# A thirteenth column pair in the stage of seven quarter products, one plain unit ahead of the attention, and another dealing of filler matmuls

## The chip, the cores and the metric

The kernel runs on one core of a Trainium2 chip. A core has TensorE (PE, matrix products into PSUM, the accumulation memory), VectorE (DVE), ScalarE (ACT) and GpSimd (POOL), and SyncE (SP), whose queue issues nearly all DMAs here. Each engine works through its own instructions in order, and semaphores tie them together. The metric is the device time of one execution in microseconds (us); a second figure, the span, runs from the first to the last instruction of the program in the profiled execution.

## The reference

One layer of an encoder over 1024 new frames and 64 frames of a running stream (1088 columns in all), with 512 cached positions. All numbers are float32.

```python
h = rms_norm(x, norm_w) @ w_in                       # 1024 -> 6144 columns
sb_q, sb_k, sb_v, sb_z, cb_q, cb_k, cb_v, cb_z, g_sb, g_cb = split(h)
# sb: stick breaking, 8 heads x 64, causal over all earlier keys
A[t, s] = beta[t, s] * prod_{s<j<t} (1 - beta[t, j]),  beta = sigmoid(q.k / 8)
# cb: softmax over a band of 9 chunks of 64 keys with a relative bias
b_sb = (o_sb * silu(z_sb)) @ w_proj_sb ;  b_cb = (o_cb * silu(z_cb)) @ w_proj_cb
y = x + (sigmoid(g_sb) * b_sb + sigmoid(g_cb) * b_cb) @ w_out
```

The last 1024 columns of `w_in` are the gate g_cb: eight units of 128 columns. The gate g_sb is eight more.

## The kernel before

A float32 operand is cut into a high and a low part, and each product is three matmuls (high x high, high x low, low x high). The stages follow one another on PE:

1. Norm and the projections that need rows by token (up to 227.5 us in the profile).
2. The stage of pairs (line 625 on): `pairs` lists 12 pairs of 128-column units (k, q, the two z, and the eight units of g_sb as four pairs of kind "sig"). A pair is worked as a 2x2 block product in seven quarter products instead of eight, each of 4 x 3 matmuls over two column pieces (256 and 288), so 168 matmuls, with sums of operands and results on DVE. `emit` (565) evaluates a finished quarter: for "sig" an ACT sigmoid into an `hl` tile (four of them) and stores. The halves of the weights are loaded ahead by `load_raw`; after the last pair it loads unit 0 of the next list. `LEAD` = 5 quarter products lie between the cutting of a weight (`prep`, `presum`) and its use.
3. `units` lists the eight units of g_cb. `run_fill` (775) makes them in the plain way: three column chunks `ci` of 24 matmuls (two of 384 columns, one of 320), 72 a unit. When a chunk is done `ev_act` copies it out and stores it. At the first matmul of chunk 1 the next unit's weights are cut (`W.split`: ACT makes the high part, line 115, POOL the low one, 122) and those of the one after it are loaded. Its generator goes on into `proj_sb`, the projection of the sb output. These are the fillers: `fill(n)` (985) emits the next n of them wherever the schedule calls it.
4. Ahead of the attention (1174 on): six times `fill(24)`, then `flush()` (pending stores), then one load: q of the sample, k, q of the first columns, v and z.
5. The attention: 136 steps, 17 for each of four head pairs in sb, then in cb. Of a pair, step one is the sample (t = 8, 576 keys), then t = 0 to 7 (blocks of 128 queries), each for head 0 and head 1. In sb block t has 128(t+1) keys, in cb at most 640. In step i the program emits: (cb) the exponentials of step i-1 and the scaling of step i-2 on ACT; the scores of step i (`qk`, `z`, line 1033; the cb bias and minimum on DVE); (sb) the scan and product of step i-1 on DVE (`mid`, 1056, 1057), which make `be`; `flush`; half of the step's fillers; a value product that has come due (`av`, 1127, with the closing product by z on DVE, `zt`, 1132); the transposes of step i-3 (`tr`, 1088), copied out of PSUM by ACT or DVE (`wT`); the other half of the fillers. A value product comes due one step after the transposes of the sample, or of head 1 of an odd t.
6. The rest of the fillers while the last outputs are loaded, then `proj_cb` and the output product.

Filler counts per step came from the step's keys (`wt`), 336 for sb in all and 287 for cb. A gate holds fillers back in the last unit until the sb outputs are stored (`late["sb"]`, at t = 1, head 1 of the first cb pair): before, when the unit before the last is complete. In the last unit the outputs `d_o` are loaded (`load_og`) and cut by ACT and POOL or DVE (`og_hi`, `og_lo`) in the steps of the fillers (`og_step`).

Of the kernel before, what the change touches and what calls it, by code (L numbers as in the profile page):

```python
# [10 lines left out]
AF = mybir.ActivationFunctionType  # L11
# [6 lines left out]
KT = 8  # L18
# [14 lines left out]
def hybrid_step_kernel(ctx: ExitStack, tc: tile.TileContext, x_prompt, x_sample, c_sbk, c_sbv, c_cbk, c_cbv,  # L33
# [111 lines left out]
    pairs = []  # L145
# [4 lines left out]
    pairs += [("sig", 4096 + 128 * j, d_g["sb"][j:j + 2]) for j in range(0, KT, 2)]  # L150
    units = [("ev_act", 5120 + 128 * j, (AF.Copy, d_g["cb"][j])) for j in range(KT)]

# [391 lines left out]
    with ExitStack() as ph:  # L544
# [20 lines left out]
        def emit(i, w, half, c, src, ps):  # L565
# [209 lines left out]
    def run_fill():  # L775
        for j, (kind, c, args) in enumerate(units):
            wh, wl = W.sp.pop(("u", j))
            for ci, (a, b) in enumerate(CH):
                ps = psF.tile([128, 512], F32, name="acc")
                for k in range(KT):  # L780
                    for n, (w, x) in enumerate(((wh, 0), (wh, 1), (wl, 0))):
                        TE.matmul(ps[:, :b - a], w[:, k], xk(x, k)[:, a:b], start=k == 0 and n == 0,  # L782
                                  stop=k == KT - 1 and n == 2)
# [324 lines left out]
    def av(b, p, j):  # L1108
        o = psO.tile([128, 256], F32, name="o")
        vp, vs = VP[b, p]  # L1110
        if j == 4:
            nq = 64
            steps = [(kb, 0, 64) for kb in range(5)]
        else:
            nq = 256
            lo = 2 * j - 3 if b == "cb" else 0
            steps = [(kb, 0, 256) for kb in range(max(0, lo), 2 * j + 1)]
            if lo > 0:
                steps.append((lo - 1, 0, 128))
            steps.append((2 * j + 1, 128, 256))  # L1120
        base = wbase(b, j)
# [59 lines left out]
    n_sb = 72 * 5 - 24  # L1181
    n_cb = 72 * (len(units) - 2) - n_sb + FP
    wt = {"sb": lambda n: n, "cb": lambda n: n + 150}
    tot = {b: sum(wt[b](band(b, t)[1]) for bb, p, t, hd in seq if bb == b) for b in ("sb", "cb")}
    amount = {"sb": n_sb, "cb": n_cb}
    acc, emitted = 0.0, 0
    LAG = 3
    avq = []
    for i in range(len(seq) + LAG + 1):
        m = 0  # L1190
# [13 lines left out]
        if i < len(seq):  # L1204
            qk(i)
            if hd == 0:
                if t % 2 == 1 or t == 8 and (b, p) != ("sb", 0):
                    load_z(b, p, t // 2 if t < 8 else 4)
                prefetch(b, p, t)
            acc += amount[b] * wt[b](band(b, t)[1]) / tot[b]  # L1210
            if (b, p, t) == ("cb", 0, 8):
                acc += 12
            m = int(acc) - emitted
            emitted += m
        if 0 < i <= len(seq) and seq[i - 1][0] == "sb":
# [305 lines left out]
```

## Time and profile before

| | us |
|---|---|
| median of three runs | 986.17 (985.58 to 986.71) |
| the profiled execution | 986.78 |
| its span | 985.0 |
| stage of pairs, PE | 227.5 to 483.0 |
| plain units ahead of the attention, PE | 483.0 to 506.7 |
| sb attention, first scores to first cb scores | 506.7 to 673.6 |
| cb attention, to the last value product | 673.6 to 832 |

A row of a stretch gives its length, then busy time and, in brackets, the number of instructions of each engine. In the order of time a row is start, duration, engine, line, operation and tiles; in square brackets the idle time ahead of it and what ended it. PE's busy time includes the tail of each matmul, so that short waits are hidden in it. "PEld" is a weight load, "SPq" the issue of a DMA.

### The profile page before, as it was taken

To read this page: it belongs to the slowest core of one execution; us is meant where nothing else is said; L and a number is where in the kernel's file an instruction comes from. 1 tells how busy PE (TensorE), PEld (TensorE's weight loads), DVE (VectorE), ACT (ScalarE), POOL (GpSimd) and SP (SyncE) were. 2 spreads that over 40 slices of the span, in tenths; PEclk is the share of its full clock that TensorE was granted. 3 is DMA by queue.
4 is the path that set the end of the run, shared out by engine and by line. 5 is a ranking of instruction groups with operands and counts; after the bars stand their busy time and mean duration, and the time that the engine had idled before them with its cause. 6 is when DMAs were issued, how large, how long until landed. Compare 5 with 4: busy or idle time off the path is not lost.

```text
span 985.0 us, 20439 instructions
## 1 busy us (share of the span) xinstructions
PE 962.0 (98%) x7568; PEld 917.6 (93%) x7568; DVE 630.1 (64%) x1188; ACT 510.4 (52%) x1142; POOL 346.2 (35%) x356
## 2 busy tenths in 40 slices
PE   5999999999999999999999999999999999999998
PEld 5999999999999999999998888898888888999998
DVE  5456665696454655532239898997767765599735
ACT  5534443344443433433248787786876875466220
POOL 3376664115444554444211101101201101486641
PEclk9999999999999999999999999999999999999999
DMA  6727567533656333343298656666898772852642
GB/s 229 223 89 243 193 223 253 166 103 120 180 174 203 115 110 101 99 124 99 79 244 221 172 160 161 164 187 169 232 262 226 213 221 68 264 177 83 210 131 86
DMA packets 174243, 166.97 MB, mean 170 GB/s; under 512 B 34688, under 2 KB 160000, under 8 KB 174016
## 3 DMA queue, kind: packets, MB, share of 16 engines
q1 hardware_dynamic: 165424, 157.34, 53.7%
q10 hardware_dynamic: 8720, 8.33, 2.6%
q8 instruction: 60, 0.98, 0.4%
q14 instruction: 39, 0.32, 0.1%
HBM read 106.89 MB, written 58.72 MB: 168 GB/s over the span
## 4 chain that ended last, share of the span: by engine, by line
PE 90%; DMA 3%; ACT 3%; DVE 1%; SPq 1%; issue 1%; POOL 1%; DVEq 0%; ACTq 0%
PE b L634 25%; PE acc L464 19%; PE b L1435 8%; PE o L1127 7%; PE acc L782 7%; PE z L1033 6%; PE pt L1088 6%; PE b L924 5%; PE acc L882 3%; DMA wrawx<-in_w_in_dram 1%; PE pk L349 1%; ACT wT L1097 1%; PE pt L277 1%; SPq L51 1%; PE acc L1471 1%
## 5 line engine op out<-in xcount | busy, mean ns | idle before, releaser
L122 POOL TENSOR_TENSOR wlo<-wraw,whi 128x1024 fp32r<-128x1024 f32 x22 | 57.6, 2618 | 103.0 <-ACT whi L115 102.9
L1088 PE MATMUL pt<-ident,be 128*128 128x128 f32 (+1 forms) x568 | 87.2, 278 | 5.7 <-ACT wT L1097 1.9
L1056 DVE TENSOR_TENSOR_SCAN kp<-kp,imp 128x128 f32<-128x128 f32 (+7 forms) x64 | 88.3, 1379 | 0.6 <-ACT kp L1036 0.6
L1033 PE MATMUL z<-ks,sq 128*128 128x320 f32 (+5 forms) x384 | 83.2, 325 | 0.0
L1088 PEld LDWEIGHTS pt<-ident,be 128*128 128x128 f32 (+1 forms) x568 | 65.9, 140 | 16.8 <-issue 5.7
L1097 ACT ACTIVATE wT<-pt 128x512 f32<-128x512 f32 (+3 forms) x125 | 58.6, 501 | 39.0 <-PE pt L1088 38.9
L464 PE MATMUL acc<-whi,xa 128*128 128x256 f32 x256 | 74.2, 292 | 0.0
L464 PE MATMUL acc<-wlox,xm 128*128 128x256 f32 x256 | 70.8, 278 | 0.0
L464 PE MATMUL acc<-whi,xm 128*128 128x256 f32 x256 | 70.8, 278 | 0.0
L464 PE MATMUL acc<-wlo,xa 128*128 128x256 f32 x256 | 70.7, 278 | 0.0
L464 PE MATMUL acc<-whix,xb 128*128 128x256 f32 x256 | 70.7, 278 | 0.0
L464 PE MATMUL acc<-whix,xm 128*128 128x256 f32 x256 | 70.6, 278 | 0.0
L1033 PEld LDWEIGHTS z<-ks,sq 128*128 128x128 f32 x384 | 65.8, 188 | 1.1 <-issue 0.2
L1127 PE MATMUL o<-wT,vp 128*64 128x256 f32 (+1 forms) x608 | 66.7, 357 | 0.1
L782 PE MATMUL acc<-xm,whi 128*128 128x384 f32 (+1 forms) x192 | 65.2, 340 | 0.0
L1127 PEld LDWEIGHTS o<-wT,vp 128*64 128x64 f32 x608 | 42.3, 136 | 23.9 <-issue 5.7
L1057 DVE TENSOR_TENSOR be<-be,kp 128x128 f32<-128x128 f32 (+8 forms) x68 | 57.3, 843 | 9.4 <-ACT sg L757 0.5
L1036 ACT ACTIVATE kp<-z 128x384 f32<-128x384 f32 (+6 forms) x104 | 52.4, 504 | 9.5 <-PE z L1033 4.5
L642 DVE TENSOR_TENSOR u<-b,s 128x256 f32<-128x256 f32 (+1 forms) x48 | 20.8, 439 | 56.3 <-PE b L634 55.2
L1037 ACT ACTIVATE be<-z 128x384 f32<-128x384 f32 (+6 forms) x104 | 52.9, 508 | 0.0
L1060 ACT ACTIVATE be<-be,sm 128x640 f32<-128x640 f32 (+5 forms) x68 | 47.2, 694 | 9.5 <-DVE sm L1059 9.2
L1047 ACT ACTIVATE be<-be,sm 128x640 f32<-128x640 f32 (+5 forms) x68 | 47.2, 694 | 3.7 <-DVE sm L1039 3.4
(300 smaller groups left out, 3147.4 us busy)
## 6 DMA issues: line engine op xcount, KB each, us to landing
wraw<-in_w_in_dram SPq DMA_DIRECT2D x32, 512.0 KB, 4.6
wrawx<-in_w_in_dram SPq DMA_DIRECT2D x16, 512.0 KB, 4.5
sq<-d_qsbT SPq DMA_DIRECT2D x32, 192.0 KB, 3.6
sq<-d_qcbT SPq DMA_DIRECT2D x32, 192.0 KB, 4.4
xt<-in_x_prompt_dram SPq DMA_DIRECT2D x8, 512.0 KB, 5.8
d_kcbT<-hl SPq DMA_DIRECT2D x8, 512.0 KB, 4.4
d_qcbT<-hl SPq DMA_DIRECT2D x8, 512.0 KB, 5.7
d_ksbT<-hl SPq DMA_DIRECT2D x16, 256.0 KB, 2.5
```

The lines of the kernel that those rows point to most:

```text
L122: (eng or G).tensor_tensor(out=l, in0=raw, in1=h[:].bitcast(F32), op=OP.subtract)
L464: TE.matmul(ps, x, w, start=m == 0, stop=m == len(steps) - 1)
L634: TE.matmul(ps[:, :m], w[:, hl_, k], right[s](x)[:, k, a:b], start=s < 3 and k == 0 and e == 0, stop=k == 3 and e == 2, skip_group_check=s ...
L782: TE.matmul(ps[:, :b - a], w[:, k], xk(x, k)[:, a:b], start=k == 0 and n == 0, stop=k == KT - 1 and n == 2)
L1033: TE.matmul(z[:, :m], s[:, e, q0:q0 + 128], ks[:, h, o + x:o + y], start=e == parts[0][0], stop=e == parts[-1][0])
L1037: A.activation(be[:r, x:y], z[:r, :m], AF.Sigmoid, scale=0.125)
L1056: V.tensor_tensor_scan(kp[:r, n - 1::-1], kp[:r, n - 1::-1], im[:, ::-1], 0.0, op0=OP.mult, op1=OP.add)
L1057: V.tensor_tensor(out=be[:r, :n], in0=be[:r, :n], in1=kp[:r, 1:n + 1], op=OP.mult)
L1088: TE.transpose(pt[:kr, x, :r], be[:r, kb * 128:kb * 128 + kr], ident[:r, :r])
L1097: A.activation(w[:, sl:sl + m, q0:q0 + r], pt[:, :m, :r], AF.Copy)
L1127: TE.matmul(o[hd * 64:hd * 64 + 64, c0:c1], vv[:kr, kb, hd * 64:hd * 64 + 64], wT[b, p, j, hd, s // 4][:kr, s % 4, c0:c1] if j < 4 else wT ...
L1435: TE.matmul(ps[:, t], left[s](xs_, k)[:, ts_], wt_[:, k], start=s < 3 and t == k == e == 0, stop=k == 3 and e == 2, skip_group_check=s > 2 ...
```

## The change

Two of the eight g_cb units move into the stage of pairs, as a thirteenth pair of a new kind "copy" (the ACT function is Copy instead of Sigmoid; the rest is as for "sig"). Six plain units are left. The six fills ahead of the attention are of 12 matmuls in place of 24, so one unit. The gate is now in chunks, and opens one chunk later: fillers stop after chunk 0 of the last unit, and the load of the sb outputs moves from the first matmul of that unit to the first one of its chunk 1. In the attention sb gets 312 fillers and cb 228, dealt by a new rule: each step has an estimate of PE's own work (scores, transposes and value product) and one of the other engine's (sb: DVE's scan and product of the step before, 3.6 ns a key and 350; cb: 1.45 ns a key and 900); a step's fillers make up the difference, times a factor that is searched so that the total fits.

```diff
+    pairs += [("copy", 5120 + 128 * j, d_g["cb"][j:j + 2]) for j in range(0, 2, 2)]
+    units = [("ev_act", 5120 + 128 * j, (AF.Copy, d_g["cb"][j])) for j in range(2, KT)]
-            if kind in ("sig", "silu"):
+            if kind in ("sig", "silu", "copy"):
-                A.activation(sg[:, :n], src[:, :n], AF.Sigmoid)
+                A.activation(sg[:, :n], src[:, :n], AF.Copy if kind == "copy" else AF.Sigmoid)
...
-                        if ci == k == n == 0 and j + 1 == len(units):
+                        if ci == 1 and k == n == 0 and j + 1 == len(units):
                             load_og("sb", 0, late["y"])
...
-                            if ci == 2:
-                                prog[0] = j
+                            prog[0] = 3 * j + ci
...
-            if prog[0] == len(units) - 2 and "sb" not in late:
+            if prog[0] == 3 * len(units) - 3 and "sb" not in late:
...
-        fill(24)
+        fill(12)
...
+    def share(i):
+        b, p, t, hd = seq[i]
+        n = band(b, t)[1]
+        pe, v = (4 if t == 8 else 2) * n / 2.2, n * 1.45 + 900
+        if i >= LAG:
+            pe += 109 * ((band(*seq[i - LAG][::2])[1] + 127) // 128)
+        if i > LAG and closes(i - LAG - 1):
+            b2, _, t2, _ = seq[i - LAG - 1]
+            pe += sum(432 * (z - y) / 256 for _, y, z in av_steps(b2, t2 // 2 if t2 < 8 else 4))
+        if b == "sb":
+            v = 350 + (band(*seq[i - 1][::2])[1] * 3.6 if i else 0)
+        return pe, v
+
+    plan = {}
+    for b, budget in (("sb", 72 * (len(units) - 1) - 48), ("cb", 48 + FP)):
...
+            for i in steps:
+                pe, v = share(i)
+                bal = max(bal + mul * v - pe, -1500)
+                got.append(max(0, int(bal / 165)))
+                bal -= 165 * got[-1]
...
+            m = plan[i]
```

Worked out by the two rules, the fillers of the 17 steps of a pair are:

| step (t, head) | 8 | 0 | 0' | 1 | 1' | 2 | 2' | 3 | 3' | 4 | 4' | 5 | 5' | 6 | 6' | 7 | 7' |
|---|---|---|---|---|---|---|---|---|---|---|---|---|---|---|---|---|---|
| sb, first pair, before | 4 | 2 | 1 | 2 | 2 | 3 | 4 | 4 | 4 | 6 | 5 | 7 | 7 | 7 | 8 | 9 | 8 |
| sb, first pair, after | 0 | 7 | 4 | 0 | 1 | 4 | 6 | 6 | 3 | 6 | 8 | 8 | 0 | 9 | 10 | 10 | 0 |
| sb, third pair, before | 5 | 2 | 1 | 2 | 2 | 3 | 4 | 4 | 4 | 6 | 5 | 7 | 7 | 7 | 8 | 9 | 8 |
| sb, third pair, after | 9 | 7 | 0 | 0 | 0 | 0 | 2 | 5 | 3 | 7 | 8 | 7 | 1 | 8 | 11 | 9 | 0 |
| cb, first pair, before | 16 | 2 | 2 | 2 | 3 | 3 | 4 | 4 | 4 | 5 | 5 | 5 | 5 | 5 | 5 | 5 | 6 |
| cb, first pair, after | 1 | 1 | 2 | 0 | 0 | 1 | 7 | 8 | 2 | 8 | 6 | 7 | 0 | 3 | 6 | 6 | 0 |
| cb, third pair, before | 4 | 2 | 2 | 2 | 3 | 3 | 4 | 4 | 4 | 5 | 5 | 5 | 5 | 5 | 5 | 5 | 6 |
| cb, third pair, after | 0 | 0 | 2 | 0 | 0 | 2 | 7 | 7 | 3 | 8 | 6 | 7 | 0 | 3 | 6 | 6 | 0 |

(0' is head 1 of t = 0.) In the first four cb steps after the change the gate holds the four fillers back until t = 1, head 1. What is not emitted in the attention, 97 fillers before and 108 after, follows behind it.

More of the change, by code (lines that the diff above doesn't have):

```diff
@@ L150, in hybrid_step_kernel @@
     pairs += [("sig", 4096 + 128 * j, d_g["sb"][j:j + 2]) for j in range(0, KT, 2)]
-    units = [("ev_act", 5120 + 128 * j, (AF.Copy, d_g["cb"][j])) for j in range(KT)]
+    pairs += [("copy", 5120 + 128 * j, d_g["cb"][j:j + 2]) for j in range(0, 2, 2)]
+    units = [("ev_act", 5120 + 128 * j, (AF.Copy, d_g["cb"][j])) for j in range(2, KT)]
     def put_t(dst, src):
@@ L1112, in av @@
             nq = 64
-            steps = [(kb, 0, 64) for kb in range(5)]
         else:
             nq = 256
[L1116 to L1120, printed above, removed]
+        steps = av_steps(b, j)
         base = wbase(b, j)
@@ L1180, in hybrid_step_kernel, with av_steps, closes @@
     FP = 180
[L1181 to L1186, printed above, removed]
     LAG = 3
     avq = []
+    def av_steps(b, j):
+        if j == 4:
+            return [(kb, 0, 64) for kb in range(5)]
+        lo = 2 * j - 3 if b == "cb" else 0
+        steps = [(kb, 0, 256) for kb in range(max(0, lo), 2 * j + 1)]
+        if lo > 0:
+            steps.append((lo - 1, 0, 128))
+        return steps + [(2 * j + 1, 128, 256)]
+    def closes(i):
+        t, hd = seq[i][2:]
+        return t == 8 or hd == 1 and t % 2 == 1
+    def share(i):
[12 more added lines that the diff above has]
+    for b, budget in (("sb", 72 * (len(units) - 1) - 48), ("cb", 48 + FP)):
+        steps = [i for i in range(len(seq)) if seq[i][0] == b]
+        lo, hi = 0.5, 6.0
+        for _ in range(40):
+            mul = (lo + hi) / 2
+            bal, got = 0.0, []
+            for i in steps:
[3 more added lines that the diff above has]
+                bal -= 165 * got[-1]
+            if sum(got) <= budget:
+                lo, best = mul, got
+            else:
+                hi = mul
+        plan.update(zip(steps, best))
+        plan[steps[-1]] += budget - sum(best)
     for i in range(len(seq) + LAG + 1):
@@ L1209, in hybrid_step_kernel @@
                 prefetch(b, p, t)
[L1210 to L1214, printed above, removed]
+            m = plan[i]
         if 0 < i <= len(seq) and seq[i - 1][0] == "sb":
```

## The prediction

> **What bounds the kernel now.** I read the page's busy times first, then the busy time of each stretch, then the order of time inside the attention.
>
> ```profile
> PE 962.0 (98%) x7568; PEld 917.6 (93%) x7568; DVE 630.1 (64%) x1188; ACT 510.4 (52%) x1142; POOL 346.2 (35%) x356
> 543.71:587.16 43.45, 42.97 (x319) 37.17 (x318) 38.33 (x40) 33.50 (x83) 3.87 (x18) 1.00 0.63 168
> 587.16:630.35 43.19, 42.49 (x318) 36.95 (x318) 39.75 (x40) 34.67 (x85) 8.53 (x19) 1.00 0.67 175
> 753.00:789.39 36.39, 36.09 (x284) 31.53 (x283) 26.32 (x101) 26.87 (x60) 2.98 (x5) 1.00 0.85 227
> ```
>
> TensorE (PE) looks like the only bound. Rows two and three are the second and third head pair of the stick-breaking (sb) attention, row four the third pair of the band (cb) attention; after the length come PE, weight loads, VectorE (DVE), ScalarE (ACT), POOL, clock, DMA share, GB/s. In an sb pair DVE is nearly as full as PE, and fuller than it looks:
>
> ```profile
> 557.20 0.96 DVE L1056 TENSOR_TENSOR_SCAN kp<-kp,imp 128x384 f32<-128x384 f32 x1
> 558.29 0.56 DVE L1057 TENSOR_TENSOR be<-be,kp 128x384 f32<-128x384 f32 x1
> 559.13 2.38 POOL L122 TENSOR_TENSOR wlo<-wraw,whi 128x1024 fp32r<-128x1024 f32 x1 [6.90 <-ACT whi L115]
> 559.46 2.87 DVE L1056 TENSOR_TENSOR_SCAN kp<-kp,imp 128x384 f32<-128x384 f32 x1 [0.61 <-ACT kp L1036]
> 553.62 0.42 DVE L1132 TENSOR_TENSOR zt<-o,zt 128x256 f32<-128x256 f32 x1 [1.55 <-PE o L1127]
> DVE zt L1132 <- PE o L1127: 5.2, 5, 1.6
> ```
>
> Between a scan and its product DVE always stands 0.13 us (557.20+0.96 to 558.29): 17 times a pair, 2.3 us. So the pair at 543.71 holds 38.3+2.3 = 40.6 of 43.4 us of DVE work, the next 42.0 of 43.2. DVE's free time is the wait for the value product (o), 1.55 us at 553.62. And a POOL weight split beside a scan takes 1.9 us of DVE (2.87 against 0.96). Taking matmuls out of sb thus frees PE, while DVE goes on setting the pace.
>
> **The change part by part.** Step and unit names are as above; E is the end of the stage of pairs, 483.0 now.
>
> *The thirteenth pair* adds 168 matmuls to a stage where PE never waits:
>
> ```profile
> 301.28 181.86 PE b L634 x1464
> 482.98 0.33 PE L782 MATMUL acc<-xa,whi 128*128 128x384 f32 x1
> 494.82 0.34 PE L782 MATMUL acc<-xa,whi 128*128 128x384 f32 x1
> ```
>
> 181.86/1464 is 0.1242 us each, so **+20.9 us**. Its Copies, sums and stores lie beside PE as those of the twelve do. One thing is new: load_unit(0), issued in the twelfth pair, takes a wraw slot whose half matrix the thirteenth pair still has to sum. SP waits there for DVE, some four quarter products (24 x 0.1242 = 3.0 us each), and behind it are the stores that free four hl tiles; only if ACT then waits too long for such a tile does PE stop. 0 to +3; I take 0, since the weights are cut five quarter products ahead.
>
> A plain unit is 494.82 - 482.98 = 11.84 us, 0.1644 per matmul. Of 144 that leave the plain units, 72 leave the stretch ahead of the attention, 24 sb (336 to 312), 59 cb (287 to 228), and 11 more come after it: -23.7 in all, if each counted. Against +20.9 that would be -2.8. I think few count.
>
> *Ahead of the attention.* The stretch is a cover for loads:
>
> ```profile
> 485.15 2.43 SPq L51 DMA_DIRECT2D kss<-d_csbT  x4
> 490.86 2.48 SPq L51 DMA_DIRECT2D sqs<-d_qsbT  x4
> 493.38 0.59 SPq L109 DMA_DIRECT2D wraw<-in_w_in_dram  x1
> 495.65 2.39 SPq L51 DMA_DIRECT2D ks<-d_ksbT  x4
> 499.19 2.48 SPq L51 DMA_DIRECT2D sq<-d_qsbT  x4
> 503.06 0.97 SPq L736 DMA_DIRECT2D vs<-in_cache_sb_v_dram  x1
> 504.08 0.52 SPq L737 DMA_DIRECT2D vs<-d_sbv  x1
> DMA to landing us min/median/max: 6.4/6.8/7.2
> 491.00:495.00 4.00, 4.00 (x29) 4.00 (x28) 0.00 (x0) 0.49 (x1) 0.30 (x1) 1.00 0.34 97
> 503.00:507.00 4.00, 4.00 (x30) 4.00 (x29) 0.00 (x0) 0.53 (x2) 0.27 (x4) 1.00 1.11 290
> 506.71 1.22 PE L1033 MATMUL z<-kss,sqs 128*128 128x288 f32 x8
> 508.47 0.33 PE L1033 MATMUL z<-ks,sq 128*128 128x128 f32 x2
> 512.20 0.95 PE L1127 MATMUL o<-wT,vs 128*64 128x64 f32 x20
> ```
>
> SP issues without a pause, 0.6 us a DMA, and DMA goes from a share of 0.34 to 1.11 (the landing row is vs'): the last of vs lands at about 504.08+6.4 = 510.5, and its first use is 512.20, 1.7 us later. With one unit fewer SP still starts at E+2.15, passes kss and sqs, then one store, ks, the weights of the unit after next, and sq: sq is issued at E+13.4 to 15.8 in place of E+16.2 to 18.7. The bytes in front are nearly the same (2.56 in place of 2.72 MB, done 12.7 us after their first issue now), so sq lands at E+20 to 21.8 and vs at about E+26 (now E+27.5). PE is done with the unit at E+11.8 and with the first scores at E+12.9, no filler stands in step 0, and it waits some 7 us for sq and again for vs. The first value product starts near E+26.2 in place of E+29.2. Of 11.8 us removed, 3.0 are left. Bounds: 11.8 (all landed in time) and 1.5 (vs' own gain). Behind the waiting PE stand scores and so ACT and DVE, which wait with it; sq of the next columns, late next, comes 2.3 us of transfers after vs and is just in time.
>
> From there to the value product that closes pair 0 (553.62, E+70.6, now) the dealing puts 86 fillers where 80 were, +1.0, and takes two from just ahead of that product and the wait of its transposes:
>
> ```profile
> 548.54 1.07 PE L1088 MATMUL pt<-ident,be 128*128 128x128 f32 x8 [0.35 <-ACT wT L1097]
> 550.11 3.46 PE L1127 MATMUL o<-wT,vp 128*64 128x256 f32 x32
> ```
>
> That is -0.8: **-2.8 us** in all by that point, E+67.8.
>
> *The sb pairs.* From one such product to the next are 44.0 and 42.8 us now. Each loses 7 or 8 fillers (1.2 us), mostly from the steps just round the product, where DVE waits for PE; and of the five weight splits that fall into sb now (filler 24, 96, 168, 240, 312 of it) four remain, one a pair. DVE work is then about 38.6+1.9 = 40.5 a pair, PE's 42.8-1.2 = 41.6: 41.8 each, **-3.2** (bounds 0 and -5). In the last stretch, into cb, 45.2 us now, 37 fillers go. PE would gain 6.1; but DVE has to finish its scans. It loses one slowed scan (-1.9) and half of its wait: **-2.8** (0 and -6.1).
>
> *The cb pairs.* Fillers leave the steps after a pair's last value product and go to the long steps:
>
> ```profile
> 752.76 0.28 ACT L1097 ACTIVATE wT<-pt 128x128 f32<-128x128 f32 x1 [2.31 <-PE pt L1088]
> 755.98 0.83 ACT L1060 ACTIVATE be<-be,sm 128x640 f32<-128x640 f32 x1 [0.21 <-DVE sm L1059]
> 757.14 0.77 PE L1088 MATMUL pt<-ident,be 128*128 128x128 f32 x5
> 715.75 0.52 ACT L843 ACTIVATE xa<-ot 128x384 fp32r<-128x384 f32 x1 [2.28 <-DMA ot<-d_osb]
> ```
>
> There PE already waits for ACT: ACT stands 2.31 us behind the product, then has two exponentials and scalings (0.8 us each) ahead of the transposes at 757.14. By that chain they can start at 756.3 at the earliest, 0.8 sooner, though ten fillers (1.7 us) go; and with no filler between the next transposes and the next product another 0.3 is lost. So 0.5 a pair for three pairs, 0.3 for the first. Against that stands the moved load of d_o: it is now issued one filler ahead of the ACT copy that reads it, not 24, so ACT stands for the load with the next exponentials queued behind it, and PE's transposes behind those. In row 715.75 such a wait cost ACT 2.28; I take 2 (0 to 3). The sum for cb is **0** (-6.3 if each of 38 fillers counts, +3).
>
> *After the attention* 11 more fillers, +1.8, against a wait that they cover:
>
> ```profile
> PE acc L882 <- DVE xm L886: 1.3, 1, 1.3
> ```
>
> **+0.4** (0 to 1.8).
>
> Sum: +20.9 - 2.8 - 3.2 - 2.8 + 0 + 0.4 = **+12.5**. The profiled execution had a span of 985.0 and took 986.8; the median shown is 986.2, 1.2 above that span. 985.0 + 12.5 + 1.2 = 998.7; I say **998.5 us**.
>
> **The rivals.**
>
> *Clock.* PE had a long rest at the start, and then:
>
> ```profile
> PEclk9999999999999999999999999999999999999999
> 11.70 1.22 PE L464 MATMUL acc<-whi,xs 128*128 128x256 f32 x4 [2.16 <-ACT whi L115]
> 15.28 0.77 PE L464 MATMUL acc<-wlo,xs 128*128 128x256 f32 x4
> ```
>
> Without the tail of a last matmul (0.28, the mean of one) that is 0.31 us a matmul at 11.70 and 0.16 at 15.28: 3.6 us at half speed. If the 7 us wait for sq puts PE back there, it loses 1.8 us, a second time after vs at most: 1000.3 for one. Before, no wait inside the span was long enough to tell.
> The Trainium skill ("TensorE: Matmul & The Clock Gate", section "Part 1: The HAM clock gate") says that an idle window of about 3.4 us halves TensorE's clock until about as much of sustained work has passed; by that rule the prologue speaks against this change and 1000.3 would be the time. The trace agrees at its start, and shows the clock granted from then on.
>
> *The loads are there in time.* If sq and vs land by the time PE asks (for it: SP never waits, and fewer bytes compete; against: the share of 1.11), DVE starts at E+13.7 and needs, as now, 39.8 us (508.5 to 548.4) to the transposes at 548.54; pair 0 then closes at E+58.8, 9 us earlier than in my sum: 989.5.
>
> *PE alone decides* (the other side). If a filler in the attention counts fully wherever it stands, and the loads are in time, it is +20.9 - 23.7: 983.4, faster. For it: 98% busy, and small waits. Against: DVE's 42.0 of 43.2. It decides from the point where DVE and ACT finish ahead of each transposition.
>
> *The chains of cb* turn worse: ACT's wait for d_o at +3, each pair 0.5 slower rather than faster: 1003.
>
> **How the numbers follow.** Forecast 0.58, clock 0.12, loads in time 0.13, PE alone 0.09, cb 0.08. The range runs from 988.0, the loads in time with some of cb's gain, to 1003.0: outside are PE alone and the upper half of cb's case. A difference under 0.2% (2 us) can't be told from none. Faster 0.10 (PE alone and a little of the loads), same 0.05, slower 0.85.
>
> **What would show it.** Right: the stage of pairs 20.9 us longer; PE idle for several us between its first scores and the next, released by a DMA of sq, and again ahead of the first value product; sb pairs of about 41.8 us with PE waits for DVE or ACT ahead of transposes; four splits in sb; an ACT wait for d_o at the first cb steps. Wrong: no PE gap after E+12.9, sb pairs under 41 us, or cb pairs under 35 us.

## The result, and the profile after

The changed kernel takes 1009.8 us (median of four runs, 1008.6 to 1011.3) against 986.4 for the kernel before beside it: a ratio of 1.023, 95% interval 1.021 to 1.026. The forecast was 998.5 with a range to 1003.0. The sign was right, and of the loss it gave half.

The page of the changed kernel, its busy times and the clock in 40 slices:

```profile
PE 965.6 (96%) x7592; PEld 923.8 (92%) x7592; DVE 634.0 (63%) x1202; ACT 513.4 (51%) x1151; POOL 348.5 (35%) x361
PEclk9999999999999999999979999999899999999999
```

PE is busy 3.6 us longer (965.6 against 962.0) in a span that is 24.5 longer (1009.5), and the clock has two dents that it did not have. The stretches of the changed kernel (length, then busy times, clock, DMA share and GB/s as in the prediction's rows): the pairs, the unit ahead, from the first scores to the first value product, the first head pair of cb, its second and third, and the stretch from the last value product to the last filler.

```profile
225.89:502.45 276.56, 276.56 (x2226) 275.69 (x2225) 125.34 (x246) 107.43 (x246) 130.86 (x91) 1.00 0.42 127
502.45:514.28 11.83, 11.83 (x74) 11.83 (x73) 1.94 (x4) 2.38 (x4) 4.44 (x7) 1.00 0.35 103
514.28:531.62 17.34, 6.83 (x35) 6.41 (x33) 4.24 (x7) 3.85 (x14) 0.30 (x3) 0.70 1.02 245
689.59:738.28 48.69, 39.84 (x290) 33.09 (x289) 27.16 (x93) 33.61 (x76) 7.80 (x10) 0.93 0.70 192
738.28:774.08 35.80, 34.52 (x273) 31.10 (x272) 27.22 (x101) 26.17 (x59) 3.84 (x6) 1.00 0.86 234
774.08:809.85 35.77, 34.44 (x274) 30.64 (x272) 26.55 (x99) 26.18 (x59) 2.99 (x5) 1.00 0.85 233
852.30:874.80 22.50, 19.59 (x111) 19.10 (x110) 7.64 (x13) 6.68 (x11) 6.64 (x5) 0.92 0.63 194
```

The same stretches of the kernel before, as far as the prediction does not show them (the pairs, first scores to first value product, first and second head pair of cb, the end):

```profile
227.38:482.98 255.60, 255.60 (x2058) 254.73 (x2057) 119.20 (x232) 99.56 (x229) 121.45 (x84) 1.00 0.43 129
506.71:512.20 5.49, 4.65 (x34) 4.14 (x32) 3.25 (x6) 3.96 (x14) 0.20 (x2) 1.00 0.96 244
673.55:714.26 40.71, 40.09 (x311) 35.34 (x311) 26.81 (x92) 31.03 (x70) 5.93 (x8) 1.00 0.63 182
714.26:753.00 38.74, 37.20 (x284) 32.37 (x283) 27.82 (x102) 29.03 (x69) 5.69 (x8) 1.00 0.83 239
831.80:849.30 17.50, 16.19 (x101) 15.75 (x100) 7.58 (x13) 4.99 (x9) 7.08 (x5) 1.00 0.68 207
```

The pairs are 20.96 us longer. The unit taken from ahead of the attention (23.73 to 11.83) comes back whole in the next stretch (5.49 to 17.34): the first value product stands 29.2 us after the end of the pairs, E, in both kernels. The first head pair of cb is 8.0 longer, the end 5.0. In those three stretches the clock falls to 0.70, 0.93 and 0.92; before it was 1.00 in each.

**The start.** What PE and SP waited for there in the changed kernel, the landing times of q, SP's issues (start, duration, what, how many), the scores that need q, the first value product, and a stretch of the clock:

```profile
PEld z L1033 <- DMA sq<-d_qsbT: 10.3, 1, 10.3
SPq L736 <- DMA wraw<-in_w_in_dram: 2.2, 1, 2.2
SPq L737 <- DMA sq<-d_qsbT: 0.6, 1, 0.6
DMA to landing us min/median/max: 8.1/8.4/8.6
515.64 0.59 SPq L109 DMA_DIRECT2D wraw<-in_w_in_dram  x1
516.27 2.70 SPq L51 DMA_DIRECT2D sq<-d_qsbT  x4
519.08 2.52 SPq L696 DMA_DIRECT2D d_gcb<-sg  x3
523.76 0.37 SPq L736 DMA_DIRECT2D vp<-d_sbv  x1
524.72 0.38 SPq L737 DMA_DIRECT2D vs<-in_cache_sb_v_dram  x1
525.56 0.66 PE L1033 MATMUL z<-ks,sq 128*128 128x128 f32 x2 [10.06 <-DMA d_gcb<-sg]
531.62 0.95 PE L1122 MATMUL o<-wT,vs 128*64 128x64 f32 x20 [0.45 <-ACT wT L1097]
519.60:529.84 10.24, 4.28 (x15) 4.31 (x16) 1.19 (x4) 0.89 (x4) 0.10 (x1) 0.50 1.06 256
```

PE waits 10 us for q. In its row at 525.56 the wait is put down to a store (d_gcb) that ended near it; the weight load beside it, in the first row, names q. SP issued q from 516.27 on, and each of the four loads took 8.1 to 8.6 us to land. And SP does not run ahead freely: values (vp) wait for a weight load, the next one for a part of q. Count the issues: wraw, four of q, three stores is eight, then vp; the load after vp waits for the first of q, again eight back. The first value product then waits for ACT's copy of a transpose, no longer for a load. The last row is the price on top: 10.24 us at half speed, in 4.28 of which PE worked.

This start differs from one execution to the next. Three kernels shown below have the same program up to the end of sb (more fillers ahead of the end, fewer in cb, and without the bias loads); in their traces the first value product stands at E+27.7, E+28.1 and E+28.0.

**The first head pair of cb.** ACT and PE of the changed kernel in order of time, and SP's issues before:

```profile
704.26 0.43 SPq L109 DMA_DIRECT2D wraw<-in_w_proj_sb_dram  x1
704.79 2.46 SPq L51 DMA_DIRECT2D ks<-d_kcbT  x4
708.11 0.54 SPq L839 DMA_DIRECT2D ot<-d_osb  x1
717.02 0.52 ACT L843 ACTIVATE xa<-ot 128x384 fp32r<-128x384 f32 x1 [4.66 <-DMA ot<-d_osb]
719.02 0.66 PE L1088 MATMUL pt<-ident,be 128*128 128x128 f32 x4 [3.22 <-ACT be L1060]
721.74 0.52 ACT L843 ACTIVATE xa<-ot 128x384 fp32r<-128x384 f32 x1 [2.78 <-DMA ot<-d_osb]
723.38 0.90 PE L1033 MATMUL z<-ks,sq 128*128 128x320 f32 x2 [2.82 <-DVE sm L1039]
721.00:727.83 6.83, 4.45 (x18) 2.70 (x18) 3.22 (x12) 5.29 (x11) 1.91 (x6) 0.50 0.92 276
```

The load of d_o issued at 708.11 is read at 717.02, 8.9 us later: the next pair's keys and a weight load were issued just ahead. ACT stands 4.66 and 2.78 us, PE 3.22 and 2.82 behind it, and from 721.00 on, within PE's second rest, the clock is at half speed for 6.83 us.

**The end.** DVE and PE of the changed kernel:

```profile
DVE og L848 <- ACT og L843: 3.8, 1, 3.8
869.64 0.41 PE L882 MATMUL acc<-xa,whi 128*128 128x320 f32 x1 [2.91 <-DVE xm L886]
871.20:874.60 3.40, 3.40 (x15) 3.40 (x14) 0.49 (x1) 1.47 (x2) 0.00 (x0) 0.50 0.86 262
```

DVE stood 3.8 us for ACT, which stood for a part of d_o, ahead of emptying the accumulators; PE stood 2.9 behind it with fillers still to come, and half speed followed.

### The profile page after: what moved, and what is told of

The parts are those of the page before. It is cut to its first block, busy times and chain, and to the rows that moved or that the text cites. A ratio compares the mean times of both kernels' runs of the same rounds, so it can differ in the third digit from the quotient of the medians.

```text
span 1009.5 us, 20537 instructions
## 1 busy us (share of the span) xinstructions
PE 965.6 (96%) x7592; PEld 923.8 (92%) x7592; DVE 634.0 (63%) x1202; ACT 513.4 (51%) x1151; POOL 348.5 (35%) x361
## 4 chain that ended last, share of the span: by engine, by line
PE 86%; DMA 4%; SPq 3%; DVE 2%; ACT 2%; issue 1%; POOL 0%; DVEq 0%; ACTq 0%
PE b L635 27%; PE acc L465 19%; PE b L1465 8%; PE o L1122 7%; PE pt L1088 5%; PE z L1033 5%; PE b L924 5%; PE acc L783 4%; PE acc L882 4%; SPq L51 2%; DVE kp L1056 1%; DMA ks<-d_kcbT 1%; DMA gt<-d_gsb 1%; PE pk L350 1%; DMA wrawx<-in_w_in_dram 1%
## 5 line engine op out<-in xcount | busy, mean ns | idle before, releaser
L1033 PE MATMUL z<-ks,sq 128*128 128x320 f32 (+5 forms) x384 | 86.9, 335 | 12.9 <-DMA d_gcb<-sg 10.1
L122 POOL TENSOR_TENSOR wlo<-wraw,whi 128x1024 fp32r<-128x1024 f32 x20 | 48.8, 2442 | 119.4 <-ACT whi L115 119.3
L1122 PE MATMUL o<-wT,vp 128*64 128x256 f32 (+1 forms) x608 | 70.3, 363 | 0.6 <-ACT wT L1097 0.6
L1122 PEld LDWEIGHTS o<-wT,vp 128*64 128x64 f32 x608 | 48.4, 139 | 22.3 <-issue 4.8
L643 DVE TENSOR_TENSOR u<-b,s 128x256 f32<-128x256 f32 (+1 forms) x52 | 22.6, 440 | 66.7 <-PE b L635 61.6
L1060 ACT ACTIVATE be<-be,sm 128x640 f32<-128x640 f32 (+5 forms) x68 | 47.2, 694 | 12.1 <-DVE sm L1059 11.9
L1022 POOL MEMSET kp<- 128x1 f32 x68 | 6.2, 98 | 125.6 <-DVE be L1057 122.5
L783 PE MATMUL acc<-xm,whi 128*128 128x384 f32 (+1 forms) x144 | 49.2, 342 | 0.0
```

Source lines behind the costliest of these rows:

```text
L1033: TE.matmul(z[:, :m], s[:, e, q0:q0 + 128], ks[:, h, o + x:o + y], start=e == parts[0][0], stop=e == parts[-1][0])
L1122: TE.matmul(o[hd * 64:hd * 64 + 64, c0:c1], vv[:kr, kb, hd * 64:hd * 64 + 64], wT[b, p, j, hd, s // 4][:kr, s % 4, c0:c1] if j < 4 else wT ...
```

## The experiments

Ratios are to runs of the kernel before on the same chip, with 95% intervals. A difference from the changed kernel is one of medians, and some are from different chips, on which the kernel before took 986.4 to 988.5 us; of such a difference under 2 us the times alone cannot say that it is real.

**The pair alone.** The kernel before gets the thirteenth pair and the six units, and nothing else. One number in its plan changes: the 144 matmuls that the pair replaces leave sb.

```diff
+    pairs += [("copy", 5120 + 128 * j, d_g["cb"][j:j + 2]) for j in range(0, 2, 2)]
-    units = [... for j in range(KT)]
+    units = [... for j in range(2, KT)]
-    n_sb = 72 * 5 - 24
+    n_sb = 72 * 3 - 24
```

> The kernel before with the thirteenth pair alone: ten units of the same kind instead of sixteen half-width ones' full set, the two units ahead of the attention (144 matmuls), the old dealing, the old gate and the old place of the loads; the 144 fill matmuls that the pair makes needless are all taken out of the sequential branch (192 there instead of 336). Theory A, the sequential branch is bound by the chain of each step on VectorE and not by TensorE, so its fill is free: pairs +20.9, the branch's four head pairs as long as before within 2 us, nothing else changed: 1005 to 1009 us. Rival B, TensorE decides there: 144 matmuls by about 0.165 us come back, some 24 us, and the time is 981 to 987 us.

Measured: 1009.2 us, 1.022 (1.020 to 1.023). The loss of the whole change, from this part alone. Its second and third sb pair:

```profile
561.88:604.22 42.34, 38.78 (x282) 32.68 (x282) 36.42 (x40) 31.71 (x81) 1.69 (x17) 0.96 0.61 156
604.22:648.61 44.39, 39.60 (x284) 34.13 (x283) 37.88 (x40) 32.44 (x83) 4.74 (x18) 0.92 0.60 152
```

Compare them with the prediction's rows at 543.71 and 587.16: 35 matmuls fewer a pair, some 5.8 us of TensorE time, and the lengths are 42.34 and 44.39 in place of 43.45 and 43.19. All four pairs together fell from 166.8 to 165.8 us: of 23.7 us freed, 1.0 came back. PE now idles 3.6 and 4.8 us, and its clock falls: in the four pairs it is at half speed for 17.1 us. That can have cost 8.5 us at most, so 14 of the 23.7 are missing even then, and rival B is out. Theory A was right on the branch; the time is 0.2 above its range, and the first two head pairs of cb are 1.6 and 2.1 us longer, which it did not expect.

**The dealing alone.** The kernel before with the new plan (336 and 288 fillers).

```diff
-            acc += amount[b] * wt[b](band(b, t)[1]) / tot[b]
...
-            m = int(acc) - emitted
-            emitted += m
+            m = plan[i]
```

> The kernel before with the new dealing alone, 336 fill matmuls over the sequential branch and 288 over the other. Theory A, the new plan gives the last step of the sequential branch and the first four of the other none, where TensorE then stands and waits for the softmax chain: the first head pair of the second branch 3 to 6 us longer, the others 1 to 3 us shorter in all, 986 to 991 us. Rival B, the dealing is worth what it was meant for and the loss in the changed kernel comes from other edits: 980 to 985 us.

Measured: 993.2 us, 1.005 (1.004 to 1.007). Its first head pair of cb:

```profile
673.85:716.68 42.83, 39.93 (x303) 34.57 (x302) 28.53 (x92) 32.09 (x70) 5.26 (x7) 0.96 0.71 190
```

Slower than either theory said: 2.1 us more than before here, with the clock at 0.96, and 3.1, 1.1 and 1.8 more in the pairs after it (the last to its last value product), where A expected a gain. sb as a whole is 1.0 shorter.

**The old dealing in the changed kernel** (312 fillers in sb by keys, 216 and 12 in cb).

> The changed kernel with the dealing alone undone: fillers by the step's keys as before, 312 in sb and 228 in cb. Theory A (the dealing is worth little; loads and the gate cost the time): sb pairs within 1 us of the change's 42.8, 41.6; the wait for q at the start is the same but for 4 fillers that now stand in front of it (0.7 us less rest); 1005 to 1012. Theory B (the new dealing is what costs): at least 8 us less, under 1002. Theory C (the new dealing is a gain that the other parts hide): over 1013.

Measured: 1005.9 us, 1.018 (1.016 to 1.020), 3.8 less than the changed kernel. The first head pair of cb:

```profile
689.38:734.38 45.00, 39.49 (x297) 32.85 (x296) 28.84 (x94) 33.83 (x77) 8.97 (x11) 1.00 0.65 189
```

3.7 us shorter, at full clock. ACT still waits for the late d_o, but in six pieces (6.1 us in all, the longest 2.0), and no half speed follows. The time is in A's range and in none of the others; but the second and third sb pair, at 42.5 and 43.6 us, are not both within A's 1 us.

**The load and the gate put back** (load of d_o at chunk 0, the gate one chunk earlier, 24 fillers from sb to cb).

```diff
-                        if ci == 1 and k == n == 0 and j + 1 == len(units):
+                        if ci == k == n == 0 and j + 1 == len(units):
...
-            if prog[0] == 3 * len(units) - 3 and "sb" not in late:
+            if prog[0] == 3 * len(units) - 4 and "sb" not in late:
```

> The changed kernel with one part undone: the sb outputs are loaded at the first matmul of the last plain unit again, and the gate stands in front of that unit (24 fillers move from sb, 288, to cb, 252). Theory A (the moved load: it is read one filler after its issue, its successor stands behind the weights and the next pair's k in DMA, ACT waits for it with the exponentials behind it, PE rests and its clock is halved): the waits of ACT for ot in the first cb pair shrink from 8 us to under 3, no halved clock after 700 us, and the time falls by 7 to 11, to 999 to 1003. Theory B (the dealing, which leaves the first cb steps without fillers, makes PE wait for ACT whatever is loaded): the rest at the sixth to eighth step of the third block stays, and the time is within 2 of 1009.8.

Measured: 1008.7 us, 1.021 (1.019 to 1.024). In the profiled execution:

```profile
687.95:732.14 44.19, 39.28 (x294) 33.49 (x293) 29.26 (x93) 33.21 (x74) 7.02 (x9) 0.96 0.64 179
695.80 1.94 PE L1088 MATMUL pt<-ident,be 128*128 128x128 f32 x8 [3.71 <-DVE be L1057]
```

The stretch is 4.5 us shorter and ACT waits 0.7 us for d_o. But the second row shows what takes the place of that wait: in the first steps of cb there is no filler, PE stands 3.7 us for DVE, and 3.4 us of half speed follow. The next pair is 2.0 longer, the two after it 1.5 together, so that cb as a whole is 1.0 shorter. A had the wait right and missed the time, which is in B's range; B's cause, first steps without fillers, shows as well, though earlier than B said and in a wait for DVE.

**Two units ahead again** (72 fillers from sb, all else as changed).

```diff
-        fill(12)
+        fill(24)
...
-    for b, budget in (("sb", 72 * (len(units) - 1) - 48), ("cb", 48 + FP)):
+    for b, budget in (("sb", 72 * (len(units) - 2) - 48), ("cb", 48 + FP)):
```

> The changed kernel with two units (six times 24) ahead of the attention again and 240 fillers in sb instead of 312; the number of matmuls is the same. Theory A (the unit that was taken away only covered loads; what PE does there costs no time, and sb is paced by DVE): the first value product starts at 29 us after the stage of pairs as in both kernels, no halved clock there, and the time falls by what 72 fillers fewer leave in sb: sb pairs of 40 to 41 us in place of 42 to 43, in all 3 to 8 us, 1002 to 1007. Theory B (PE alone decides, each filler counts alike wherever it stands): only the halved clock goes, 1.8 to 5 us; and theory C (the first steps of the dealing make the wait, not the missing unit): PE still waits for q some us after its first scores, and the time stays within 2 of 1009.8.

Measured: 1016.4 us, 1.029 (1.026 to 1.031), slower. Ahead of the attention, and from the first scores to the first value product:

```profile
502.75:526.48 23.73, 23.73 (x146) 23.73 (x145) 1.94 (x4) 4.75 (x8) 6.83 (x8) 1.00 0.71 192
526.48:531.97 5.49, 4.48 (x33) 4.07 (x31) 3.25 (x6) 3.85 (x14) 0.20 (x2) 1.00 1.13 284
```

The first value product stands at E+29.2 again, now without a wait and at full clock: with a unit less it stood at E+27.7 to E+29.2 in the four traces named above, so of the 11.8 us taken out 0 to 1.5 were saved there. The 72 matmuls fewer in sb gained nothing either, and the first head pair of cb is 3.3 us longer. A was right on this start and missed the time, which went the other way; B and C missed it too.

**The weights later.** In the changed kernel the 0.5 MB load of the unit after next goes behind q and v in unit 0.

```diff
-                        if ci == 1 and k == 0 and n == 0:
+                        if ci == (1 if j else 2) and k == 0 and n == 0:
                             if j + 2 < len(units):
                                 load_unit(j + 2)
```

> The changed kernel with the 0.5 MB weight load of the first unit issued one column chunk later, that is behind the queries and values of the first head pair. Theory A, the start of the attention is bound by its transfers: the queries land 2 to 4 us earlier and the first value product stands at 25 to 27 us after the end of the pairs instead of 29.2; the time falls to 1005 to 1008 us. Rival B, something else (the eight transfers in flight, whatever they carry, or the values alone) sets it: first value product at 28.5 or later, 1008.5 to 1011 us.

Measured: 1006.3 us, 1.019 (1.018 to 1.021), 3.5 less. The first value product, E = 502.39:

```profile
528.23 0.95 PE L1123 MATMUL o<-wT,vs 128*64 128x64 f32 x20 [0.45 <-ACT wT L1098]
```

E+25.8 in place of E+27.7 to E+29.2, as A said. The four loads of q landed faster:

```profile
DMA to landing us min/median/max: 5.4/5.7/5.9
```

So the transfers ahead of q are at least a part of what sets the start.

**The same edit in the kernel before.**

> The kernel before with the 0.5 MB weight load of the first unit behind the values of the first head pair. Theory A, in this kernel TensorE's two units (23.7 us) and the 5.5 us from the first scores set the first value product, with the transfers just in time: still E+29.2, 985 to 988 us. Rival B, the transfers set it here too: E+25 to E+27, 982 to 985 us, faster than both kernels.

Measured: 991.2 us, 1.003 (1.001 to 1.004). The first value product is at E+29.2 still, so A holds there: two units and 5.5 us of chain set it. The time did not fall but rose a little, above both ranges. The trace is level with the kernel before from the close of the first sb pair to the second head pair of cb, which then takes 40.52 us (38.74), with a wait of 1.9 us for ACT and 3.4 us of half speed in it; why, no run tells.

**More fillers ahead, with the transfers as they were** (12, 12, 12, 12, 36, 36 in place of six times 12; 264 in sb).

> The changed kernel with 120 instead of 72 fill matmuls ahead of the attention (12 ahead of each of the first four loads as now, then 36 and 36) and 264 instead of 312 in the sequential branch; transfers as they were. Theory A, transfers set the first value product (E is the end of the pairs): it stays at E+27 to E+29.5 though TensorE starts the scores 7.9 us later, the half-speed stretch of 10.24 us becomes 3.4 us or none, and the first head pair loses 1.5 to 3 us by that: 1006 to 1009 us. Rival B, TensorE's own work and not the transfers set it: E+34 or later, and the time 1011 us or more.

Measured: 1014.7 us, 1.028 (1.026 to 1.030). The first value product is at E+29.8 and only 3.4 us of half speed are left, yet the second head pair starts at E+61.6 (61.2 in the changed kernel). The run does not isolate the clock: the next weight cut now falls into this stretch, and ACT stands 4.7 us for its load. The first head pair of cb is 51.0 us long, close to the 52.0 with two units ahead. Theory A misses the time; B has it, but not the place of the value product that it rests on.

**More fillers ahead of the end** (57 in place of 46 before the first part of d_o).

> The changed kernel with 57 fillers in place of 46 ahead of the first cutting of the cb outputs behind the attention (then 24, and 27 in place of 38 at the end). Theory A (DVE stands for the second load of d_o ahead of emptying PSUM, PE rests for it with 38 fillers still to go; fillers ahead of that point are free): the rest of 2.9 us at the end goes or halves and the last stretch of 22.5 us takes 19 to 20.5: 1006.5 to 1008.5. Theory B (the load lands late whatever is in front): the stretch stays at 22 to 23, 1009 to 1011.

Measured: 1008.9 us, 1.022 (1.019 to 1.024). The end:

```profile
851.20:871.58 20.38, 18.63 (x112) 18.20 (x111) 8.60 (x13) 5.05 (x9) 6.44 (x5) 0.97 0.61 186
```

2.1 us shorter in the trace, as A said, with PE's wait for DVE 1.8 in place of 2.9. Half speed still comes, from 870.35 on, and so mostly behind this stretch: what follows is 1.0 us longer than in the changed kernel. The time, 0.9 lower, lies between the two theories and is not told from none.

**The single repairs together** (old dealing, gate and load, 57 ahead of the end).

> The changed kernel with the old dealing, the old gate and place of the loads, and eleven more fill matmuls ahead of the first part of the end: the three single edits gave 3.8, 1.1 and 0.9 us alone. Theory A, they act at different places and add: 1002 to 1005 us, with the first head pair of the second branch at 41 to 43 us. Rival B, the dealing and the gate mend the same stall: 1004.5 to 1007 us.

Measured: 1004.3 us, 1.017 (1.015 to 1.019), within A's range by the time and 0.2 below B's. But the first head pair of cb took 45.9 us, above A's 41 to 43: 2.8 less than in the changed kernel, and less gained than by the dealing alone (3.7) or the load and the gate alone (4.5). By that the two mend the same stall, as B said. With the late weights besides:

> The kernel with the old dealing, the old gate and eleven more fill matmuls in the end (1004.3 us) and the 0.5 MB weight load behind the first values besides, which alone gave 3.5 us. Theory A, it adds 2 to 3.5 us: 1000.5 to 1002.5 us. Rival B, its start of the attention was short already (first value product at E+26.4 against E+25.8 with the late load alone): 1003.5 to 1005 us.

Measured: 1005.7 us, 1.020 (1.017 to 1.022): nothing added, and above both ranges. The first value product came at E+24.7, but the first head pair of cb grew to 46.9 us with twice the half speed.

**All repairs, first try** (120 fillers ahead as above, late weights, old dealing 216 and 288, old gate).

> The changed kernel with the repairs together: 120 fill matmuls ahead of the attention, the weight load of 0.5 MB behind the first values, the old dealing (216 and 288, so that 24 remain for the change of branch), the old gate and the old place of the loads, 96 fill matmuls left for the end as before. Theory A, what is left of the loss is the pair itself against chains of fixed length: first value product at E+25.5 to 26.5, head pairs of the first branch at 42 to 43, end (from the last value product to the last fill) 17 to 18 us: 995 to 1001 us, still slower than before. Rival B, the freed TensorE time comes back once the stalls are gone: 983 to 988 us.

Measured: 1013.6 us, 1.027 (1.024 to 1.029). What ACT waited for at the start:

```profile
ACT whi L115 <- DMA wraw<-in_w_in_dram: 10.1, 1, 10.1
```

With 120 fillers ahead the cut of the next weights comes before their late load has landed. ACT stands 10.1 us with the softmax queued behind it; the first value product is at E+34.4. The repair made a new wait, and both theories missed.

**All repairs, second try** (72 ahead, 264 and 288).

> The changed kernel with 72 fill matmuls ahead as it has, the 0.5 MB weight load behind the first values, the old dealing (264 and 288, so that 24 are left for the change of branch), the old gate and place of the loads, 96 for the end. Theory A, the repairs add once no load stands in ScalarE's way: first value product at E+25.5 to 26.5, head pairs of the first branch 42 to 43, the first of the second branch 41.5 to 43, the end 17 to 18.5: 999 to 1003 us, slower than before still. Rival B, what one place gives the next takes: 1004 to 1010 us as in the single repairs.

Measured: 1007.9 us, 1.021 (1.020 to 1.023). Its second sb pair and the first head pair of cb:

```profile
561.97:603.64 41.67, 40.13 (x301) 34.26 (x300) 37.29 (x39) 32.95 (x83) 4.43 (x18) 1.00 0.58 154
691.98:733.47 41.49, 40.09 (x313) 35.99 (x313) 28.65 (x93) 31.40 (x71) 5.93 (x8) 1.00 0.62 175
```

The start (E+24.6), the first head pair of cb (41.5) and the end (17.5) came out as A said or better. The total did not: the other sb pairs took up to 44.5 us with half speed in them, the second head pair of cb 40.8. Rival B was right by the time: what one place gave, the next took.

**Fewer fillers in cb** (156 in place of 228; 72 more in the end).

> The changed kernel with 156 instead of 228 fill matmuls in the second branch; the 72 follow in the emptied end, some 12 us there. Theory A, the second branch's head pairs 2 to 4 stand at the length of their own chain already: 35.0 to 35.8 us each (now 35.80, 35.77, 35.75) with TensorE idle for 3 us or more in each, so the time rises by 8 to 13 us to 1018 to 1023 us. Rival B, TensorE sets them: 33 to 34.3 us each, and the time is 1008 to 1013 us.

Measured: 1016.6 us, 1.031 (1.028 to 1.034). And the same **without the bias loads** of head pairs 2 to 4:

> The kernel with 156 fill matmuls in the second branch, and without the loads of the bias tables of head pairs 2 to 4, about 1 MB of some 8 MB that each of the pairs 2 and 3 moves (the first pair's tables are used in their place, so the output is another). Theory A, with little fill the pairs 2 and 3 stand at 36.4 and 35.7 us because of their transfers (DMA share 0.85): they fall by 2 us or more each, to 32 to 34 us. Rival B, the chain of the steps sets them: within 0.6 us of 36.4 and 35.7.

Measured: 1010.4 us, 1.025 (1.023 to 1.027). Pairs 2 and 3 of the first of these kernels, and then of the second:

```profile
732.50:768.88 36.38, 33.85 (x255) 27.42 (x253) 26.28 (x100) 26.83 (x64) 1.90 (x6) 1.00 0.85 229
768.88:804.61 35.73, 31.97 (x251) 27.63 (x252) 25.27 (x96) 25.45 (x58) 3.29 (x6) 1.00 0.86 227
```

```profile
730.41:765.21 34.80, 32.83 (x255) 27.30 (x253) 26.10 (x99) 26.81 (x63) 4.14 (x3) 1.00 0.84 225
765.21:798.79 33.58, 31.79 (x254) 27.62 (x253) 25.18 (x97) 25.17 (x58) 0.00 (x0) 1.00 0.83 209
```

18 or 23 matmuls fewer left pairs 2 and 3 where they were in the changed kernel (35.80, 35.77), with PE idle up to 3.8 us; so theory A of the first kernel is nearly right there (36.38 is above its range). The time is 1.4 us below A's: the first head pair, which A left out, fell by 5.2 us, to 43.5. Less to load shortened pairs 2 and 3 by 1.6 and 2.2 us: the second kernel's A for pair 3, short of its 2 us for pair 2. The transfers are at least a part of what holds them.

## Why the sign was right and the size wrong

The closing products by z of sb pairs 0 to 3 and of the first head pair of cb in the changed kernel, in order of time:

```profile
575.09 0.42 DVE L1127 TENSOR_TENSOR zt<-o,zt 128x256 f32<-128x256 f32 x1 [1.22 <-PE o L1122]
617.00 0.42 DVE L1127 TENSOR_TENSOR zt<-o,zt 128x256 f32<-128x256 f32 x1 [0.80 <-PE o L1122]
658.68 0.43 DVE L1127 TENSOR_TENSOR zt<-o,zt 128x256 f32<-128x256 f32 x1 [0.73 <-PE o L1122]
700.57 0.42 DVE L1127 TENSOR_TENSOR zt<-o,zt 128x256 f32<-128x256 f32 x1 [3.54 <-PE o L1122]
746.13 0.42 DVE L1127 TENSOR_TENSOR zt<-o,zt 128x256 f32<-128x256 f32 x1 [1.75 <-PE o L1122]
```

The kernel before closed them at 553.62, 597.58, 640.42, 685.61 and 724.07, with E at 482.98 in place of 502.45. From these, in the prediction's own steps, us:

| step | predicted | measured |
|---|---|---|
| thirteenth pair | +20.9 | +21.0 |
| E to the close of sb pair 0 | -2.8 | +2.0 |
| the two sb pairs | -3.2 (41.8 each) | -3.2 (41.9 and 41.7) |
| last sb stretch | -2.8 | -3.3 |
| cb | 0 | +5.5 |
| end | +0.4 | +5.0 |
| ahead of the pairs, behind the end | 0 | -2.5 |
| sum | +12.5 | +24.5 |

(The last row but one lies in stages that the change leaves as they were.)

*Right: the pair, and the sb pairs.* The pairs of the changed kernel close 41.9, 41.7 and 41.9 us apart, and PE works for all but 0.4 to 0.7 us of them by their first scores, as in the prediction's sum. Fewer fillers than the changed kernel has gained nothing more. The mean of the second to fourth sb pair, from first scores to first scores, against the fillers in sb:

| kernel | fillers in sb | dealing | mean, us |
|---|---|---|---|
| before | 336 | old | 43.3 |
| the dealing alone | 336 | new | 42.6 |
| the old dealing | 312 | old | 42.9 |
| changed | 312 | new | 42.0 |
| the single repairs together | 288 | old | 42.3 |
| the load and the gate put back | 288 | new | 42.0 |
| all repairs, second try | 264 | old | 43.3 |
| more fillers ahead | 264 | new | 42.1 |
| two units ahead | 240 | new | 42.6 |
| all repairs, first try | 216 | old | 43.0 |
| the pair alone | 192 | old | 43.4 |

No kernel comes below 42.0; a single pair of 40.3 us (more fillers ahead, its second) is followed by 42.5 and 43.5. With 264 fillers or fewer each of these stretches has half speed in it, with 288 or more none has. So the first 24 to 48 fillers taken out of 336 count, by 1.3 us a pair at most, and more do not; the prediction's rival "PE alone decides" is out. That DVE sets the 42 was argued from its 38 us and its gaps; no run took work from DVE.

*The start, 4.8 off: the term "done 12.7 us after their first issue, so sq lands at E+20 to 21.8".* It took SP's pauseless issue for given and the old landing times for the transfers (4.8 to 5.0 us for q in the kernel before). With ks, weights and q issued closer together the four of q needed 8.1 to 8.6 us each and landed at E+22.3 to E+23.9; with the late weights they needed 5.4 to 5.9. And it let the values set the first value product, E+26.2. They were held back at the issue, but had landed at E+27.2, 2.0 us ahead of that product; it waited for what q releases, 6.1 us of scores, eleven fillers and transposes, the greater part of it at half speed (3.7 us from such scores on in the kernel before). So of 3.0 us of gain none was left in this trace, and 1.1 to 1.5 in the three with the same start. The other 1.8, of the 4.8, lie between the first value product and the close of the pair (43.5 us in place of 41.4), and they are the new dealing's: alone in the kernel before it makes that stretch 43.3 us, and with the old dealing the changed kernel has 41.5. The prediction gave the dealing +1.0 and -0.8 there; it is +1.9 in both comparisons. (Later pairs give it back: with the dealing alone sb as a whole is 1.0 shorter.) With the late weights the stretch is 43.5 too, though half speed ends ahead of it. The rival "the loads are there in time" is out.

*cb, 5.5 off: the term "the moved load, I take 2 (0 to 3)".* The wait was seen, its size not: it was priced by a load that landed 3.1 us after its issue, and the moved one goes behind four key loads and a weight load and took 8.9. The wait came three times, 8.1 us for ACT in all, and half speed came with it. Putting the load back shortened that head pair by 4.5 us, the old dealing alone by 3.7, both by 2.8, and both with 24 fillers left for the first steps by 7.2 (41.5 us); 19 matmuls fewer in it, with 72 fillers less in cb, took 5.2 off. So the wait and the fillers' place act together, and no run gives the wait's own share. The pairs after it gave 1.6 us back, against 1.5 forecast, but as 1.1, 0.6 and -0.1 in place of 0.5 each, and the forecast laid it to ACT's chain where the run without the bias loads points to transfers: the sum is luck in part.

*The end, 4.6 off: "11 more fillers, +1.8, against a wait that they cover".* They cover a wait ahead of them, but PE then waits for DVE, which stands for the second d_o, and half speed follows. Eleven fillers moved ahead of it gave 2.1 us in the trace, of which 1.0 was lost again behind it.

*The clock* was named as a rival for one place, at 1.8 us. It came at all three: 10.24, 6.83 and 3.41 us. PE worked in 4.28, 4.45 and 3.40 of them, and half of that, 6.1 us, is the most that it can have cost. At the start that is 2.1 us, between q and the first value product, so that rival's condition came true and its price was near; how much of the rest lay on the path, no run isolates.

*The loss as a whole.* The pair alone loses as much: 21 us of work in a stage where PE is the bound, for 24 us taken from a stage where PE was 98% busy and yet only some 1.3 us per pair (43.3 against 42.0) above the next limit. The changed kernel takes its 24 us from other places, and there the loss is the sum of the table's rows. Of the other parts the new dealing costs (3.8 us by its removal, 5.5 alone). One unit ahead is better than two by 6.6 us in the medians (1.8 in the two traces), of which an earlier first value product can be 1.5 at most; that it keeps fillers where PE would stand is argued only. Of the kernels run none beat the kernel before; the best with the thirteenth pair is 1.7% slower.

## What to carry to other kernels

A stage in which one engine is 98% busy may stand less than 5% above the next limit, so before work is moved out of it, take a little out and see whether its length follows. Work that covers waits also holds the clock: with 264 fillers or fewer, PE's rests put it at half speed, and the sb pairs gained nothing by it on the mean. A load moved nearer to its reader is to be priced behind what is issued just ahead of it, not by its price alone.

## What the runs showed of the hardware

- PE fell to half speed for stretches of 3.41, 6.83, 10.24 and once 13.65 us (the load and the gate put back), one to four times the same length. The Trainium skill ("TensorE: Matmul & The Clock Gate", section "Part 1: The HAM clock gate") gives one window of about 3.4 us for the fall and for the way back; the lengths agree. But the rest need not fill that window: half speed came after rests of 10.06 and 3.22 us, and also after 2.91 at the end of the changed kernel, 1.89 in the same edit in the kernel before and 1.75 with more fillers ahead of the end. Cut into slots of 3.41 us that fit their clock changes, the 17 traces show 50 falls within the kernel; each ends a slot in which PE rested for 1.7 us or more, and no slot without a fall holds over 1.9. By these figures a rest of about half a slot is enough, where it falls into one slot.
- SP's issue waited, in both places counted above, for the DMA issued eight before it. In the trace's records these issues wait for a semaphore of the program, the one that the DMA eight before had used: SP's DMAs take eight semaphores in turn. So the eight is the program's; whether the chip has a limit of its own, no run tells.
- How long a load takes depends on what is in the queue with it: q landed after 8.1 to 8.6 us at a DMA share of 1.06 behind the 0.5 MB of weights, after 5.4 to 5.9 ahead of them, and the load of d_o that the cb steps read was used 8.9 us after its issue.
